# A hybrid decoder block on one core: where the first mean, the gate weights and the y combinations stand, and how the last block is closed

## Chip, core and metric

One core of one Trainium2 chip. The metric is device time in microseconds (us) of one execution; a run gives one time, and the median of the runs is used. A profiled execution gives times for every instruction of the five engines (PE: TensorE matrix unit, DVE: VectorE, ACT: ScalarE, POOL: GpSimd, SP: SyncE, which here issues nearly all DMAs).

## The reference

One layer of a decoder, sequence 2048, width 1024, float32. Cut to what matters:

```python
h = rms_norm(x, norm1_g)                       # mean of squares over the 1024 channels
z = h @ w_in                                   # 1024 -> 28 blocks of 128 channels
lru_x, lru_gate, sc_b, sc_c, sc_x = split(z)   # 8, 8, 4, 4, 4 blocks
lru_x = causal_dwconv(lru_x, 4 taps) + bias
r, i = sigmoid(lru_x @ wa + ba), sigmoid(lru_x @ wx + bx)     # 64x64 heads
log_a = -8 * r * softplus(-lam)
y_lru = scan(h = a*h + sqrt(1-a*a)*i*lru_x) * gelu(lru_gate)
y_sc  = sc_b * causal_dwconv(sc_c * sc_x, 3 taps)
x = x + concat(y_lru, y_sc) @ w_out            # 12 blocks -> 8
u = causal_dwconv(rms_norm(x, norm2_g) @ w_up, 3 taps)        # 8 -> 48 blocks
x = x + (gelu(gate) * up) @ w_down             # 24 blocks -> 8
out = rms_norm(x, final_g)
```

## The kernel before

Channels lie on the 128 partitions, positions along the free axis. The sequence is worked in two halves of 1024 positions, each half in two blocks of 512. Every product is exact to float32 by splitting both factors into a high and a low part (names `wh`/`wl` for weights, `xh`/`xl`, `fh`/`fl`, `rh`/`rl` for the other factor; ACT makes the high part at L195, DVE the low part at L196), and three matmuls take the place of one. A product of the first stage has 8 steps of 6 matmuls.

The stages follow one another on PE: products with `w_in` (`in_phase`, matmuls L234), products with `w_out` in `sweeps` (L700, tiles `ox`/`oy`), both for half 0, then both for half 1; then for each half the products with `w_up` (L581) and those with `w_down` (`sweeps` again, tiles `dx`/`dy`).

`in_phase` runs through 12 units: `L` units (a gated recurrence, two products and two small gate products `zr`, `zi`) and `S` units (short convolution, three products). In half 0 the first two products, `zin_0` and `zin_8`, go along as pieces of x arrive; then come product `zin_1`, the mean of squares of x (`inv_rms`, matmuls L265 with a matrix of ones into two PSUM banks `ms_a`, then ACT L269 and DVE L270 to L272), and `zin_9`. The result of `inv_rms`, the tile `ss_a`, scales every product when it is taken out of PSUM (`evac`, L371). The recurrence needs the constants `c8` and `nc8`, which `decay_rates` works out in some 28 operations on 128x8 numbers, with one function of ACT (`dt`).

The gate weights of a recurrence (256 columns) are loaded into the raw tile (`wr`, two buffers) of one `w_in` chunk, after that chunk, and split by `gate_weights` into a tile `gw`.

`sweeps` is one level of Strassen with seven block products: per sweep `ni/2` steps (3 for `w_out`, 6 for `w_down`), each with 24 matmuls. A step loads a weight piece and a piece of the other factor into one raw tile (L711, L712), splits both into four of the ten pages of a pool, and multiplies. The sums of blocks of y or of the FFN's inner activation that Strassen needs are made once by `combine` for each pair of units and stored to DRAM (`B11`, `B21`, `B22` are blocks, `T1` to `T4` sums; `y_d`, `f_d`). Residual tiles (`xr`, `x2r`, keys 11, 12, 21, 22) are fetched at places given by the table `at`; after a sweep DVE adds its PSUM tiles to them (L735), as `TAKEN` lists. The out-product also takes along work for the next part: in half 0 `x_prep` for the next half's x (`x_1`, `xh_1`), in half 1 `h_prep`, which prepares the FFN's input (`ha`, `hb`, `hc`, `hq`, and their parts `hhB`, `hlB`, `hhT`, `hlT`, `ht`).

At the end `finish_block` scales the last four pairs of tiles (L879) by the last mean and stores them. The last square of that mean, of the tile `x2r` with m = 3, is split and fed to two matmuls of its own.

What sets the order: PE, SP and POOL issue in the program's order. On ACT and DVE a scheduler chooses by readiness and priority (`HP` 120 before `HW` 90 before `HE` 30), and the chosen order is then fixed: each engine works in order, so an instruction that waits holds up those behind it. Buffers come from pools: 28 pages `act`, 7 pages `tmp`, 10 pages for parts, 2 raw tiles, two pairs of larger tiles, 8 PSUM banks; a new tile waits for the last reader of the page that it gets. Stores are put off by `defer(n, ...)`: `tick()`, called once for each weight load, counts down and issues what is due, on SP.

## Time and profile before

| what | us |
|---|---|
| three runs | 2307.86, 2305.12, 2307.29 |
| median | 2307.29 |
| profiled execution, whole | 2304.75 |
| its span, first to last instruction | 2302.9 |
| `w_in` products, half 0 / half 1 on PE | 7.45 to 345.2 / 461.7 to 789.9 |
| `w_out` sweeps, half 0 / half 1 | 345.2 to 461.7 / 789.9 to 910.7 |
| `w_up` and `w_down`, half 0 | 910.7 to 1368, to 1597 |
| `w_up` and `w_down`, half 1 | to 2054.5, to 2287 |

The span is what the trace covers; 1.85 us of the whole time lie around it. A line of the profile's groups reads: line of the kernel, engine, operation, output tile <- input tiles, shape, how often, time, and in brackets the idle time before it with what ended it. The chain of waits is followed back from the last instruction to what released each step.

### The profile page before, as it was taken

How to read it: one execution, taken by the hardware profiler on the slowest of the kernel's cores; microseconds unless marked ns; L12 is line 12 of the kernel's file. 1: busy time of each engine (PE TensorE's matmuls, PEld its weight loads, DVE VectorE, ACT ScalarE, POOL GpSimd, SP SyncE). 2: the span in 40 equal slices, each digit the busy share in tenths (PEclk: the TensorE clock that was granted, in tenths of full speed). 3: DMA queues.
4: the chain of work that ended last, by engine and by line, in shares of the span. 5: the costliest groups of instructions: out<-in, count | busy, mean ns of one | idle time of the engine just before them, and what ended most of it. 6: DMA issues, size and time to landing. Idle time of an engine off the chain costs nothing.

```text
span 2302.9 us, 26017 instructions
## 1 busy us (share of the span) xinstructions
PE 2272.7 (99%) x9984; PEld 1875.2 (81%) x9984; DVE 1723.8 (75%) x1910; ACT 1136.0 (49%) x1242; POOL 141.4 (6%) x232
## 2 busy tenths in 40 slices
...
GB/s 182 106 141 162 80 183 243 271 177 147 195 156 143 235 246 248 102 92 114 92 114 92 114 155 289 204 242 216 87 92 115 92 119 88 122 169 324 256 186 181
DMA packets 145597, 378.28 MB, mean 164 GB/s; under 512 B 13824, under 2 KB 17024, under 8 KB 144896
## 3 DMA queue, kind: packets, MB, share of 16 engines
...
q8 instruction: 78, 1.28, 0.2%
...
## 4 chain that ended last, share of the span: by engine, by line
PE 94%; DVE 3%; DMA 1%; ACT 1%; issue 1%; SPq 0%; DVEq 0%; ACTq 0%
PE zin_b L234 25%; PE zx L581 23%; PE zc L581 11%; PE dx L700 11%; PE dy L700 8%; PE za L581 6%; PE ox L700 5%; PE oy L700 3%; PE zr_b L234 1%; PE zi_b L234 1%; DMA x<-in_xT 1%; DMA wr_d<-sd_d_S 0%; DVE x2r L879 0%; DVE cv L294 0%; DVE fl_o L196 0%
## 5 line engine op out<-in xcount | busy, mean ns | idle before, releaser
L234 PE MATMUL zin_b<-xh,wh_in 128*128 128x512 f32 x896 | 277.2, 390 | 4.8 <-DVE ss_a L270 2.6
L234 PE MATMUL zin_b<-xl,wh_in 128*128 128x512 f32 x896 | 277.0, 390 | 0.1
L234 PE MATMUL zin_b<-xh,wl_in 128*128 128x512 f32 x896 | 276.3, 390 | 0.0
L234 PEld LDWEIGHTS zin_b<-xh,wh_in 128*128 128x128 f32 x896 | 168.5, 188 | 40.9 <-DVE ss_a L270 3.5
L234 PEld LDWEIGHTS zin_b<-xl,wh_in 128*128 128x128 f32 x896 | 168.5, 188 | 36.4 <-DVE xl L402 1.7
L234 PEld LDWEIGHTS zin_b<-xh,wl_in 128*128 128x128 f32 x896 | 168.5, 188 | 35.0
L196 DVE TENSOR_TENSOR fl_d<-wr_d,fh_d 128x1024 fp32r<-128x1024 f32 x84 | 102.8, 1223 | 104.5 <-ACT fh_d L195 102.2
L195 ACT ACTIVATE fh_d<-wr_d 128x1024 fp32r<-128x1024 f32 x84 | 89.1, 1061 | 176.7 <-PE dy L700 79.7
L196 DVE TENSOR_TENSOR wla_up<-wr_up,wha_up 128x1024 fp32r<-128x1024 f32 x48 | 58.8, 1226 | 139.0 <-ACT wha_up L195 139.0
L700 PE MATMUL dx<-fl_d,wh_d 128*128 128x512 f32 x384 | 149.5, 389 | 0.8 <-DVE fl_d L196 0.8
L700 PE MATMUL dx<-fh_d,wl_d 128*128 128x512 f32 x384 | 149.4, 389 | 0.0
L700 PE MATMUL dx<-fh_d,wh_d 128*128 128x512 f32 x384 | 149.4, 389 | 0.0
L557 DVE TENSOR_TENSOR wr_up<-wr_up 128x512 f32<-128x512 f32 x192 | 130.0, 686 | 14.7 <-DMA wr_up<-in_w_up 13.5
L195 ACT ACTIVATE wh_in<-wr_in 128x1024 fp32r<-128x1024 f32 (+1 forms) x62 | 60.2, 973 | 159.1 <-DMA wr_in<-in_w_in 154.4
L196 DVE TENSOR_TENSOR wl_in<-wr_in,wh_in 128x1024 fp32r<-128x1024 f32 (+1 forms) x62 | 69.1, 1118 | 80.4 <-ACT wh_in L195 80.4
L581 PE MATMUL zc<-hhB,whd_up 128*128 128x512 f32 x384 | 126.0, 389 | 0.0
L294 DVE SCALAR_TENSOR_TENSOR cu<-un,prm,cu 128x1024 f32<-128x1024 f32 x96 | 122.7, 1278 | 4.3 <-ACT cu L290 4.3
L196 DVE TENSOR_TENSOR wl_d<-wr_d,wh_d 128x1024 fp32r<-128x1024 f32 x84 | 102.5, 1220 | 28.0 <-ACT wh_d L195 25.6
L294 DVE SCALAR_TENSOR_TENSOR cg<-ug,prm,cg 128x1024 f32<-128x1024 f32 x96 | 122.8, 1279 | 0.4
L581 PE MATMUL zx<-ht,whc_up 128*128 128x512 f32 x384 | 118.2, 389 | 0.0
L592 ACT ACTIVATE ug<-zx 128x512 f32<-128x512 f32 x96 | 57.5, 599 | 122.8 <-PE zx L581 122.6
L195 ACT ACTIVATE wh_d<-wr_d 128x1024 fp32r<-128x1024 f32 x84 | 88.4, 1053 | 59.8 <-DMA wr_d<-sd_d_S 32.0
...
## 6 DMA issues: line engine op xcount, KB each, us to landing
wr_up<-in_w_up SPq DMA_DIRECT2D x96, 512.0 KB, 4.9
wr_in<-in_w_in SPq DMA_DIRECT2D x54, 512.0 KB, 4.1
wr_d<-sd_d_S SPq DMA_DIRECT2D x48, 512.0 KB, 3.7
wr_d<-f_d_T SPq DMA_DIRECT2D x48, 512.0 KB, 4.9
f_d_B<-cu SPq DMA_DIRECT2D x72, 256.0 KB, 2.4
wr_d<-in_w_down SPq DMA_DIRECT2D x36, 512.0 KB, 3.6
wr_d<-f_d_B SPq DMA_DIRECT2D x36, 512.0 KB, 4.6
wr_o<-so_d_S SPq DMA_DIRECT2D x24, 512.0 KB, 4.5
```

The source lines that it names most:

```text
L195: nc.scalar.activation(r32(hi), src, AF.Copy)
L196: nc.vector.tensor_tensor(r32(lo), src, hi, ALU.subtract)
L234: nc.tensor.matmul(ps[t], r32(a), r32(b[:, blk(t)]), start=(first and i == 0), stop=(last and i == 2))
L294: nc.vector.scalar_tensor_tensor(dst, src[:, k : k + T], col(o_w + k), dst, ALU.mult, ALU.add)
L557: nc.vector.tensor_tensor(raw[:, o, :], raw[:, a, :], raw[:, b, :], ALU.add)
L581: nc.tensor.matmul(ps, r32(p[:, s]), r32(self.hs[k][x][o]), start=f and i == 0, stop=l and i == 2, skip_group_check=True,)
L592: nc.scalar.activation(dst, self.x, AF.Copy)
L700: nc.tensor.matmul(ps[m], r32(p), r32(x[:, k, :]), start=first and i == 0 and n == 0, stop=(last or not on_x) and i == ni - 1 and n == 2, ...
```

## The change

It has five parts.

1. In half 0 the mean is taken inside the product `zin_1`, after two of its eight steps (`product` gets a callback `mid`). The POOL copy that marks the mean's readiness writes into a column of `dz`, the first tile of `decay_rates`, and no longer into the matrix `ones`; so `decay_rates` comes after the mean.
2. The gate weights of unit c are loaded with chunk c, not with chunk 8 + c, and split at once, before the product, into a `tmp` page and no longer an `act` page. The block sums of weights that POOL adds by DMA (`sum_step`) begin one product earlier.
3. `combine` is cut in two: `combine_even` subtracts and puts `B11` and `T1` in line for storing with the even unit of a pair, `combine_odd` does the rest with the odd unit. In `in_phase` the last odd unit's stores wait 7 ticks, where they waited 5. The FFN holds the even unit's `cg` for the sum and needs no tile `tt`.
4. In `sweeps` the residual tiles 22 are fetched where those of 12 were, and those of 12 where 22 were.
5. At the end of the last sweep the additions for m = 3 get twice the priority; `finish_block` stores each 512 positions of a channel block by itself (8 stores of 256 KB each time, where it made 4 of 512 KB); and the last square is multiplied as it is, in float32, with `ones`, without a split.

```diff
-    def decay_rates():
-        z = cp.tile([P, NLRU], F32, name="dz")
+    def decay_rates(z):
...
-    def product(ps, wts, acts):
+    def product(ps, wts, acts, mid=None):
         n = len(acts)
         for k in range(n):
+            if mid is not None and k == 2:
+                mid()
             product_step(ps, wcol(wts, k), acts[k], k == 0, k == n - 1)
...
-                nc.tensor.matmul(p, ones_r, r32(x[:, blk(b)]), start=i == 0, stop=i == len(terms) - 1)
+                w, v = (ones_r, r32(x[:, blk(b)])) if i < 2 else (ones, x[:, blk(b)])
+                nc.tensor.matmul(p, w, v, start=i == 0, stop=i == len(terms) - 1)
...
-        raw = gate_raw[c]
-        gw = flat(act(f"gw{half}_{c}"))
+        gw = flat(tmp(f"gw{half}_{c}"))
...
-        product(ps, load_weights(w_in[o], f"in{half}_{o}", o - NLRU if NLRU <= o < 2 * NLRU else None), acts)
+        c = o if o < NLRU else None
+        wts = load_weights(w_in[o], f"in{half}_{o}", c)
+        if c is not None:
+            gate_w[c] = gate_weights(c, half)
+        product(ps, wts, acts, mid)
...
-    gw = gate_weights(0, half)
-    ps_2 = in_product(1, half, acts) if half == 0 else None
-    rs = inv_rms(acc, f"a{half}", parts)
-    nc.gpsimd.tensor_copy(ones[:, 0:1], rs[:, 0:1])
-    ready.append(True)
+    def mean():
+        rss.append(inv_rms(acc, f"a{half}", parts))
+        nc.gpsimd.tensor_copy(mark, rss[0][:, 0:1])
+        ready.append(True)
+    if half == 0:
+        gate_w[0] = gate_weights(0, half)
+        ps_2 = in_product(1, half, acts, mean)
...
+        last = n >= NOUT - 2
         if n % 2 == 0:
-            put(y_d[half], 5 if n < NOUT - 2 else 4, n // 2, "B11", y[:, blk(0)])
-            even = y
+            even, yc = y, flat(tmp(f"yc{half}_{n}"))
+            combine_even(y_d[half], 4 if last else 5, n // 2, even, yc)
         else:
-            combine(y_d[half], 5, n // 2, even, y, c, d)
+            combine_odd(y_d[half], 7 if last else 5, n // 2, even, y, yc, flat(tmp(f"yd{half}_{n}")))
...
+    def combine_even(dst, when, i, a, c):
+        put(dst, when, i, "B11", a[:, t0])
+        nc.vector.tensor_tensor(c[:, t0], a[:, t0], a[:, t1], ALU.subtract)
+        put(dst, when, i, "T1", c[:, t0])
...
-    ("12", ((1, 0), (1, 0))), ("22", ((1, 1), (1, 2)))
+    ("22", ((1, 0), (1, 0))), ("12", ((1, 1), (1, 2)))
...
-                    with tc.high_priority(offset=HP if last else HE):
+                    with tc.high_priority(offset=HE if not last else 2 * HP if m == 3 else HP):
...
-                    scaled(r[:, m, :], 4 * mh + 2 * p + m, rs)
-                c = 4 * mh + 2 * p
-                o = T + t * NB
-                defer(4, yT[c : c + 2, :, o : o + NB].rearrange("m p c -> p m c"), r)
+                    c = 4 * mh + 2 * p + m
+                    scaled(r[:, m, :], c, rs)
+                    defer(4, yT[c, :, T + t * NB : T + (t + 1) * NB], r[:, m, :])
...
-                terms.extend(mean_split(sq, "l2"))
+                terms.append(sq)
```

How the instructions stand, at three places. First, ACT in the first stage of half 0, around the mean of x (`wh_in_9` is the high part of chunk 9's weights, `cv_0` and `xch_0` belong to the convolution of the first recurrence); before:

```order
L195 ACTIVATE wh_in_9_606<-wr_in_9_605 128x1024
L195 ACTIVATE wh_in_20_715<-wr_in_20_714 128x1024
L269 ACT_TABLE_LOAD
L269 ACTIVATE ry_a_545<-ms_a_0_539,eps 128x512
L269 ACTIVATE ry_a_545<-ms_a_512_540,eps 128x512
L195 ACTIVATE wh_in_24_818<-wr_in_24_817 128x1024
L292 ACTIVATE cv_0_558<-xl_0_553,prm 128x1024
L195 ACTIVATE wh_in_16_882<-wr_in_16_881 128x1024
L195 ACTIVATE xch_0_563<-cv_0_558 128x1024
L195 ACTIVATE wh_in_2_948<-wr_in_2_947 128x1024
```

and now:

```order
L196 ACTIVATE gw_1_493<-wr_in_1_486 128x256
L274 ACT_TABLE_LOAD
L274 ACTIVATE ry_a_514<-ms_a_0_508,eps 128x512
L274 ACTIVATE ry_a_514<-ms_a_512_509,eps 128x512
L196 ACTIVATE wh_in_9_611<-wr_in_9_610 128x1024
L196 ACTIVATE wh_in_20_721<-wr_in_20_720 128x1024
L196 ACTIVATE wh_in_24_820<-wr_in_24_819 128x1024
L297 ACTIVATE cv_0_564<-xl_0_559,prm 128x1024
L159 ACT_TABLE_LOAD
L159 ACTIVATE dt<-dz 128x8
L196 ACTIVATE wh_in_16_884<-wr_in_16_883 128x1024
L196 ACTIVATE wh_in_2_950<-wr_in_2_949 128x1024
```

`gw_1`'s split, which stood far behind these rows, and the mean's `ry_a` now stand ahead of `wh_in_9`; the load of a function table and `dt` of `decay_rates` come in behind `cv_0`, and `wh_in_2` now stands ahead of `xch_0`, which is the next row.

Second, the queue SP in half 0's out-product, around the end of the first sweep (`wr_o_1_1` is the raw tile of sweep 1, step 1; `yc_11`, `sv_3`, `yd_11` hold the last pair of y); before:

```order
L711 DMA wr_o_1_1_2755<-so_d_S_1_212 128x1024
L712 DMA wr_o_1_1_2755<-y_d_T_1_95 128x1024
L192 DMA y_d_T_2_96<-yc_11_2579 128x512
L192 DMA y_d_T_2_99<-yc_11_2579 128x512
L192 DMA y_d_B_2_90<-sv_3_2574 128x512
L192 DMA y_d_T_2_102<-yd_11_2580 128x512
L192 DMA y_d_B_2_93<-sv_3_2574 128x512
L192 DMA y_d_T_2_105<-yd_11_2580 128x512
L509 DMA xr_22_0_2772<-in_xT 128x2x512
L400 DMA x_1_2798<-in_xT 128x1024
L711 DMA wr_o_1_2_2807<-so_d_S_2_213 128x1024
L712 DMA wr_o_1_2_2807<-y_d_T_2_96 128x1024
```

and now:

```order
L527 DMA xr_22_0_2728<-in_xT 128x2x512
L527 DMA xr_22_1_2730<-in_xT 128x2x512
L730 DMA wr_o_1_1_2756<-so_d_S_1_213 128x1024
L731 DMA wr_o_1_1_2756<-y_d_T_1_96 128x1024
L527 DMA xr_12_0_2767<-in_xT 128x2x512
L408 DMA x_1_2793<-in_xT 128x1024
L730 DMA wr_o_1_2_2802<-so_d_S_2_214 128x1024
L731 DMA wr_o_1_2_2802<-y_d_T_2_97 128x1024
L527 DMA xr_12_1_2813<-in_xT 128x2x512
L730 DMA wr_o_2_0_2847<-so_d_S_0_215 128x1024
L731 DMA wr_o_2_0_2847<-y_d_T_0_98 128x1024
L193 DMA y_d_T_2_100<-yc_10_2445 128x512
```

`x_1` and the loads of step 2 (`wr_o_1_2`) and of `wr_o_2_0` moved ahead of five stores of the last pair; the sixth (`T1`) has gone out earlier. DVE at the end of that sweep before (additions L735 of its PSUM tiles `oy`):

```order
L196 TENSOR_TENSOR fl_o_2_0_2860<-wr_o_2_0_2852,fh_o_2_0_2859 128x1024
L735 TENSOR_TENSOR xr_12_0_2727<-xr_12_0_2727,oy_1_0_2712 128x512
L735 TENSOR_TENSOR xr_22_0_2772<-xr_22_0_2772,oy_1_0_2712 128x512
L735 TENSOR_TENSOR xr_12_0_2727<-xr_12_0_2727,oy_1_1_2713 128x512
L735 TENSOR_TENSOR xr_12_1_2729<-xr_12_1_2729,oy_1_2_2714 128x512
L196 TENSOR_TENSOR wl_o_2_1_2900<-wr_o_2_1_2896,wh_o_2_1_2899 128x1024
L196 TENSOR_TENSOR fl_o_2_1_2904<-wr_o_2_1_2896,fh_o_2_1_2903 128x1024
L735 TENSOR_TENSOR xr_22_0_2772<-xr_22_0_2772,oy_1_1_2713 128x512
```

and now (L754):

```order
L197 TENSOR_TENSOR fl_o_2_0_2860<-wr_o_2_0_2847,fh_o_2_0_2859 128x1024
L754 TENSOR_TENSOR xr_12_0_2767<-xr_12_0_2767,oy_1_0_2713 128x512
L754 TENSOR_TENSOR xr_12_0_2767<-xr_12_0_2767,oy_1_1_2714 128x512
L754 TENSOR_TENSOR xr_22_0_2728<-xr_22_0_2728,oy_1_0_2713 128x512
L754 TENSOR_TENSOR xr_22_0_2728<-xr_22_0_2728,oy_1_1_2714 128x512
L754 TENSOR_TENSOR xr_12_1_2813<-xr_12_1_2813,oy_1_2_2715 128x512
L754 TENSOR_TENSOR xr_12_1_2813<-xr_12_1_2813,oy_1_3_2716 128x512
L754 TENSOR_TENSOR xr_22_1_2730<-xr_22_1_2730,oy_1_2_2715 128x512
L754 TENSOR_TENSOR xr_22_1_2730<-xr_22_1_2730,oy_1_3_2716 128x512
L410 SCALAR_TENSOR_TENSOR xl_2_2889<-x_2_2887,prm,xh_2_2888 128x1024
L197 TENSOR_TENSOR wl_o_2_1_2900<-wr_o_2_1_2896,wh_o_2_1_2899 128x1024
L197 TENSOR_TENSOR fl_o_2_1_2904<-wr_o_2_1_2896,fh_o_2_1_2903 128x1024
```

All eight additions and `xl_2` now stand ahead of `wl_o_2_1`, where four additions did.

Third, ACT in half 1's out-product, around sweep 1, step 2; before:

```order
L195 ACTIVATE fh_o_1_1_5940<-wr_o_1_1_5927 128x1024
L195 ACTIVATE hhB_1_5912<-ha_1_5900 128x1024
L195 ACTIVATE hhB_1_5916<-hb_1_5901 128x1024
L195 ACTIVATE hhT_1_5920<-hc_1_5906 128x1024
L195 ACTIVATE ht_1_5924<-hq_1_5907 128x512
L195 ACTIVATE wh_o_1_2_5973<-wr_o_1_2_5970 128x1024
L195 ACTIVATE fh_o_1_2_5977<-wr_o_1_2_5970 128x1024
```

and now:

```order
L196 ACTIVATE fh_o_1_1_5935<-wr_o_1_1_5928 128x1024
L196 ACTIVATE hhB_1_5913<-ha_1_5901 128x1024
L196 ACTIVATE wh_o_1_2_5968<-wr_o_1_2_5965 128x1024
L196 ACTIVATE hhB_1_5917<-hb_1_5902 128x1024
L196 ACTIVATE fh_o_1_2_5972<-wr_o_1_2_5965 128x1024
L196 ACTIVATE hhT_1_5921<-hc_1_5907 128x1024
L196 ACTIVATE wh_o_2_0_6018<-wr_o_2_0_6010 128x1024
```

The four parts of `h_prep`'s tiles stood together ahead of step 2's splits; now one stands ahead of `wh_o_1_2` and one between it and `fh_o_1_2`.

More of the change, by code (lines that the diff above doesn't have):

```diff
@@ L99, in block_kernel @@
     xl_halo = cp.tile([P, NLRU, 3], F32, name="xl_halo")
+    dz = cp.tile([P, NLRU], F32, name="dz")
+    mark = dz[:, 0:1]
     h_last = cp.tile([P, NLRU], F32, name="h_last")
@@ L203, in block_kernel @@
     gate_raw = {}
+    gate_w = {}
     def load_parts(src, name, parts, gate=None):
@@ L313, in gate_weights @@
     def gate_weights(c, half):
-        raw = gate_raw[c]
-        gw = flat(act(f"gw{half}_{c}"))
+        gw = flat(tmp(f"gw{half}_{c}"))
         hi, lo = gw[:, 0 : 2 * P], gw[:, 2 * P : 4 * P]
         with tc.high_priority(offset=HW):
-            split(hi, lo, raw)
+            split(hi, lo, gate_raw[c])
         return hi, lo
@@ L414, in in_phase @@
             acts = []
-            loads = [load_parts(w_in[o], f"in{half}_{o}", KC // 2, g) for o, g in ((0, None), (NLRU, 0))]
+            loads = [load_parts(w_in[o], f"in{half}_{o}", KC // 2, g) for o, g in ((0, 0), (NLRU, None))]
             wts = [None, None]
@@ L431, in in_phase @@
         parts = mean_split(acc, f"a{half}")
-        gw = gate_weights(0, half)
-        ps_2 = in_product(1, half, acts) if half == 0 else None
-        rs = inv_rms(acc, f"a{half}", parts)
-        nc.gpsimd.tensor_copy(ones[:, 0:1], rs[:, 0:1])
-        ready.append(True)
+        rss = []
+        def mean():
[5 more added lines that the diff above has]
+            ps_2 = in_product(1, half, acts, mean)
+        else:
+            ps_2 = None
+            mean()
+        rs = rss[0]
         xc, cv = lru_conv(0, half, pss[0], rs)
         if half == 0:
-            decay_rates()
+            decay_rates(dz)
         cur = (xc, cv, lru_gate(0, half, pss[1], rs))
@@ L450, in in_phase @@
                 ps_g = in_product(NLRU + nxt[1], half, acts) if n == 0 else None
-                if n > 0:
-                    gw = gate_weights(c, half)
-                gates = lru_gates(c, half, xc, gw)
+                gates = lru_gates(c, half, xc, gate_w[c])
                 if nxt[0] == "L":
```

20 lines of the change are left out of this document (9 added, 11 removed).

## The prediction

> **What bounds the kernel now.** I read the page's head and its chain first.
>
> ```profile
> span 2302.9 us, 26017 instructions
> PE 2272.7 (99%) x9984; PEld 1875.2 (81%) x9984; DVE 1723.8 (75%) x1910; ACT 1136.0 (49%) x1242; POOL 141.4 (6%) x232
> PE 94%; DVE 3%; DMA 1%; ACT 1%; issue 1%; SPq 0%; DVEq 0%; ACTq 0%
> ```
>
> PE is the bound in every stage. One row of the chain in order of time gives its pace, and one of the view of waits (total, number, longest) what mostly stops it.
>
> ```profile
> 78.81 54.40 PE zin_b L234 x240
> ```
>
> ```profile
> PE oy L700 <- DVE fl_o L196: 3.9, 3, 1.6
> ```
>
> At full pace 240 matmuls take 54.40 us, 0.2267 us each. The change takes one matmul of some 9,770 away, so only the places where PE waits can give anything. Below, a loss at a place is the distance between the starts of two matmuls less 0.2267 us, read from PE's timeline, with the slower matmul or two behind it. All such losses add up to some 24 us; work elsewhere that becomes cheaper is worth nothing.
>
> **First stage of half 0** (parts 1 and 2).
>
> ```profile
> 10.05 1.15 ACT L401 ACTIVATE xh<-x,prm 128x1024 fp32r<-128x1024 f32 x1 [0.48 <-DMA x<-in_xT]
> 11.39 0.18 DVE dt L174
> 11.75 1.29 DVE xl L402
> 13.08 30.33 PE zin_b L234 x130
> 43.41 0.69 PE ms_a L265 x3
> 44.19 1.28 ACT L269 ACT_TABLE_LOAD   x1 [4.81 <-PE ms_a L265]
> 46.20 1.30 DVE ss_a L270 x2
> 46.95 1.09 PE L234 MATMUL zin_b<-xh,wh_in 128*128 128x512 f32 x2 [2.64 <-DVE ss_a L270]
> 59.82 0.73 PE L234 MATMUL zr_b<-xch,gw 128*128 128x512 f32 x2 [1.34 <-ACT xch L195]
> 61.08 0.74 PE L234 MATMUL zr_b<-xcl,gw 128*128 128x512 f32 x2 [0.53 <-DVE xcl L196]
> 68.19 1.23 DVE L196 TENSOR_TENSOR xcl<-cv,xch 128x1024 fp32r<-128x1024 f32 x1 [1.13 <-ACT xch L195]
> 75.34 0.40 ACT L195 ACTIVATE gw<-wr_in 128x256 fp32r<-128x256 f32 x1
> 75.79 0.73 PE L234 MATMUL zr_b<-xch,gw 128*128 128x512 f32 x2 [1.23 <-ACT gw L195]
> ```
>
> - Start: `decay_rates` holds DVE in small operations of 0.18 us; without them `xl` of the second x piece starts at 11.2, when `xh` is done, and not at 11.75. PE hangs on it at 13.08: −0.6.
> - `zin_9` waits for a PSUM bank that the mean has to free: 3.3 lost at 46.95 (2.80, and 0.5 in the slow matmuls after it). Now the mean's matmuls come 36 matmuls, 8.2 us, earlier, and PE has 8.2 us of `zin_1` to do while ACT and DVE work on them. That chain took 3.3 us, from 44.1 to the end of `ss_a` L270 at 47.5. The wait goes: −3.3.
> - `zr_0` lost 2.4 in two waits for the parts of the convolution (`xch`, `xcl`). From the mean's matmuls (44.2) to `xcl_0` (61.0) the chain takes 16.9. With the mean ending at 35.7 (`zin_1` starts at 43.41 − 10.88 − 0.6 = 31.9, then two steps of 1.36 and 4 matmuls, and 0.2 to the end) it would be done at 52.6. But the 28 operations of `decay_rates`, one more table load of ACT (1.28) and one weight split now stand in it. All of DVE's added work would be 28 × 0.18 = 5.0; part of it fills pauses in which DVE waits for ACT. I take 2.7, `xcl_0` at 55.3. PE wants it at 43.41 − 0.6 + 0.9 + 10.88 + 0.45 = 55.0: 0.4 to 0.5 stay, −1.9. With nothing in the way it is −2.4, with all of it 0.
> - `zr_1` lost 1.5 (1.40 and 0.11), waiting for `gw_1`, whose split ACT reached at 75.34. It is now split before the mean. What is late next is `xcl_1`, at 69.4 before and by the same 5.7 earlier now, 63.7, plus some decay work, against PE's 54.6 + 0.5 + 2.72 + 10.88 = 68.7. It is in time: −1.5.
>
> Sum: **−7.2** (7.3, rounded toward the work added on DVE), between −4.2 (the first rival) and −8.0. Behind 78.81 PE keeps its pace through the rest of both first stages, so the earlier `gw` splits (0.40 each on ACT, their number unchanged) and the earlier `T1` gain nothing there. They cost nothing as long as the weights stay several products ahead and the seven `tmp` pages come free in time.
>
> **Out-product, half 0** (part 3).
>
> ```profile
> 361.11 7.55 DMA x<-in_xT
> 372.73 0.50 PE L700 MATMUL oy<-fh_o,wh_o 128*128 128x512 f32 x1 [0.17 <-ACT fh_o L195]
> 374.62 0.51 PE L700 MATMUL oy<-fl_o,wh_o 128*128 128x512 f32 x1 [1.38 <-DVE fl_o L196]
> 378.12 2.48 DVE L735 TENSOR_TENSOR xr<-xr,oy 128x512 f32<-128x512 f32 x4 [0.55 <-PE oy L700]
> 380.52 1.22 DVE L196 TENSOR_TENSOR wl_o<-wr_o,wh_o 128x1024 fp32r<-128x1024 f32 x1
> ```
>
> Step 2 of sweep 1 loses 0.33 + 1.66 + 0.12 = 2.1: its split stands on ACT behind `xh_1`, whose load was issued behind six stores. Five of these now stand behind the loads of this step and the next, so `x_1` is issued and lands earlier by the time of five issues: −2.1. Behind it a new wait arises. After the sweep DVE took four additions (2.48) ahead of `wl_o_2_1`; now eight (4.95) and `xl_2` (1.2). Started 1.9 us before the sweep's end, where they started here too, then 1.14 and 1.22 for the two splits, `fl_o_2_1` is ready at −1.9 + 4.95 + 1.2 + 1.14 + 1.22 = 6.6 after the end; PE needs it at 5.44 + 0.23 = 5.7. That costs 1.0 (0 if DVE gets a microsecond earlier to its additions, 2.1 if as much is lost here as at the place before). Net **−1.0**, between −2.1 and 0.
>
> **Out-product, half 1** (parts 3 and 4).
>
> ```profile
> 812.82 0.50 PE L700 MATMUL oy<-fl_o,wh_o 128*128 128x512 f32 x1 [0.90 <-DVE fl_o L196]
> 818.83 0.50 PE L700 MATMUL oy<-fh_o,wh_o 128*128 128x512 f32 x1 [0.50 <-ACT fh_o L195]
> 820.92 0.80 PE L700 MATMUL oy<-fl_o,wh_o 128*128 128x512 f32 x1 [1.59 <-DVE fl_o L196]
> 815.00:820.00 5.00, 3.83 (x16) 2.62 (x14) 5.00 (x6) 5.00 (x7) 0.00 (x0) 1.00 0.47 181
> 820.00:825.00 5.00, 4.08 (x12) 3.25 (x13) 3.14 (x3) 1.47 (x2) 0.00 (x0) 0.66 0.63 221
> ```
>
> ```profile
> L195 ACT ACTIVATE fh_d<-wr_d 128x1024 fp32r<-128x1024 f32 x84 | 89.1, 1061 | 176.7 <-PE dy L700 79.7
> ```
>
> (The windows' columns: PE, PEld, DVE, ACT, POOL busy, granted clock, DMA share, GB/s.) The wait at 812.82 stays: DVE's order ahead of it is the same. The second place loses 0.66 + 1.87 in waits, and the matmuls behind them run slowly, 0.37 + 6 × 0.2 more, together 3.9 to 4.1, of which I count 3.9. ACT and DVE were both full from 815 to 820 with the four parts of `h_prep`'s tiles ahead of step 2's splits. Now two stand ahead on ACT, one before each split. Counting the new order's rows from the same start, ACT's at the 1.06 of the last row and DVE's at 1.22, `fl_o_1_2` comes at 819.1 instead of 820.9; PE needs it at 818.2: 0.8 stay, with no slow clock behind so short a wait as the 0.90 at 812.82, which ran at 1.00 after. **−3.1**, between 0 and −3.9.
>
> [...]
>
> **Down, half 1** (part 3).
>
> ```profile
> 2060.00:2065.00 5.00, 5.00 (x23) 4.13 (x22) 4.96 (x5) 2.96 (x3) 0.00 (x0) 1.00 0.22 46
> 2075.00:2085.00 10.00, 10.00 (x46) 8.29 (x45) 4.00 (x4) 3.19 (x3) 0.00 (x0) 1.00 1.04 399
> 2105.41 0.50 PE L700 MATMUL dy<-fl_d,wh_d 128*128 128x512 f32 x1 [0.76 <-DVE fl_d L196]
> ```
>
> One step loses 1.5 (0.38 + 1.03 + 0.11), because its load lands late in a stretch in which the DMA runs full. `T1` of the last pair, 256 KB, moves from that burst to the even unit, into 2060 to 2065, where the share is 0.22. At 399 GB/s it is 0.26 MB / 0.399 = 0.65 us less ahead of the load: **−0.6**, between 0 and −1.5.
>
> **End** (part 5).
>
> ```profile
> 2287.95 0.64 ACT sq_last L913
> ...
> 2290.02 0.51 PE ms_l L265
> 2293.45 5.39 DVE L879 SCALAR_TENSOR_TENSOR x2r<-x2r,prm,ss_l 128x512 f32<-128x512 f32 x8
> 2294.89 4.35 SPq L192 DMA_DIRECT2D out_yT<-x2r  x4
> out_yT<-x2r SPq DMA_DIRECT2D x4, 512.0 KB, 2.9
> f_d_B<-cu SPq DMA_DIRECT2D x72, 256.0 KB, 2.4
> 1.00 4.54 PE L746 MATMUL warm<-ones 128*128 128x128 f32 x22 [1.00 <-POOL eps L96]
> ```
>
> From the square's end (2288.59) to the last mean's matmul (2290.53) lie 1.94. In its place stands one float32 matmul. The only such row is the last, at the start of the kernel: 11 of a quarter of the columns (two records each) in 4.54 us, 0.41 each, so 4 × 0.41 + 0.28 = 1.9 at that pace. At the pace of this kernel's matmuls, four times 0.2267 and the 0.28 that the row of 0.51 has over it, it is 1.2; I take that, since PE worked until 2286.5: −0.7, between 0 and −1.0. The doubled priority changes no order on DVE and gives nothing. The stores: the first now waits for one scaled tile of 0.67, not two, and eight issues at 4.35 / 8 or so, if an issue took half as long for half the bytes, keep up with DVE's 5.39 us: −0.7, between 0 and −0.8. **−1.4** together.
>
> **Sum:** −7.2 − 1.0 − 3.1 − 0.6 − 1.4 = −13.3. The profiled execution took 2304.75 (its span 2302.9 and 1.85 around it), which gives 2291.45. It lies 2.5 below the median of the runs, 2307.29; against that the sum gives **2294.0**.
>
> **Rivals.**
> - The first stage gives part of it back: the decay operations all lie in the way of `xcl_0`, so `zr_0` gains nothing (−5.4), and `zin_20` waits for one weight split of 1.2 behind them. Then −4.2 in place of −7.2: 2297.0. For it: from 46.2 to 61.0 DVE or what waits on it is already last in the chain. Against it: DVE has pauses there, and only `zr_0` is near its limit.
> - The sweeps give nothing: the stall moves from sweep 1 to sweep 2, and `h_prep` still has to be done on the same engines in the same stretch. Then −13.3 + 4.1 = −9.2, 2298.1. For it: DVE full from 815 to 820. Against it: ACT's order puts step 2's splits earlier.
> - Slower: `gw` in a `tmp` page. ACT works in order, and if the page's last reader is a store (of `yc` or `yd`) not landed yet, the split stops ACT, and with it the weights. It decides if the page comes free later than the weights' lead, over one product of 10.88. Eight units at a store's 2.4 us (the row of `f_d_B<-cu`) are +19; with −13.3 the time is about 2313. Against it: those stores stand on SP before the loads of the chunk concerned.
> - Stores one by one: if each of the last stores had its whole time to landing for itself, eight at 2.4 would take 19.2 against 11.6 for four at 2.9, 7.6 more: 2301.6. Against it: four of 2.9 were issued within 4.35 us, and the end lay 8 us behind the first issue, so they overlapped. [...]
> - No effect: the waits are merely taken over by the next operand everywhere. The doubled priority is of that kind. Within 4.6 us of no change.
>
> **Chances.** Forecast 0.54 (2290 to 2297.5); first stage 0.2; sweeps 0.12; stores 0.02; nothing 0.08; slower 0.04. All better ends together are −17.3, 2290.0, and the three runs of before lie 2.7 apart, some 1.4 to a side: 2288.5 is the range's lower end. The first two rivals together give −6.2, 2301: its upper end. Within it lie the forecast and these two, 0.86 in all. A measurement of this kernel can tell about 0.2%, 4.6 us, from no change: faster than 2302.7 has 0.88, within 0.08, slower 0.04.
>
> **What would show it.** In the changed profile: no wait of `zin_b` for `ss_a` near 44 and none of `zr_b` for `gw`; the second gate products near 68.5; a short wait of `oy` near 385 in half 0; one wait under 1 us near the second step in half 1; `ms_l` as one longer record and the last stores starting one tile after scaling begins. A wait of ACT for a DMA ahead of a `gw` split, or losses within the first stages after 70 us, would prove the sum wrong.

## The result, and the profile after

| | before | changed |
|---|---|---|
| median of six runs, us | 2307.43 | 2293.58 |
| lowest to highest | 2302.71 to 2309.76 | 2291.88 to 2296.08 |
| ratio, 95% interval | | 0.9944 (0.9932 to 0.9957) |
| profiled execution, us | 2304.75 | 2291.88 |
| its span, us | 2302.9 | 2290.1 |

The changed kernel is faster by 13.85 us, 0.6%. The profiled executions differ by 12.87, their spans by 12.8. The page's head, its chain (shares by engine) and, behind the marks, two rows of the view of waits (total, number, longest) of the changed kernel read:

```profile
span 2290.1 us, 26044 instructions
PE 2268.6 (99%) x9984; PEld 1873.6 (82%) x9984; DVE 1722.5 (75%) x1909; ACT 1137.2 (50%) x1242; POOL 153.4 (7%) x232
PE 88%; DVE 3%; DMA 1%; ACT 1%; issue 1%; POOL 0%; DVEq 0%; SPq 0%; ACTq 0%; POOLq 0%
...
PE oy L719 <- DVE fl_o L197: 1.5, 2, 0.9
...
PE zr_b L236 <- ACT xch L196: 1.0, 1, 1.0
```

PE is still the bound, and its busy time fell by only 4.1 us (some of the slow matmuls are gone); the rest of the 12.8 was waiting. The wait of `oy` for `fl_o` went from 3.9 us in three places to 1.5 in two. A wait of `zr_b` for `xch` is left, but not the one that the prediction spoke of, as its place in the timeline shows. Where the time went is read from the starts of the same work on PE in the two timelines:

| work on PE | before | changed | earlier by | step |
|---|---|---|---|---|
| first product after `zr_1`, `zi_1` | 78.64 | 71.27 | 7.4 | |
| first product after `zr_4`, `zi_4` | 217.36 | 212.07 | 5.3 | −2.1 |
| half 0, out-product | 345.20 | 339.91 | 5.3 | 0 |
| half 0, its sweep 4 | 412.60 | 406.30 | 6.3 | +1.0 |
| half 1, out-product | 789.78 | 783.50 | 6.3 | 0 |
| half 0, up | 910.57 | 899.92 | 10.7 | +4.4 |
| half 1, down | 2054.81 | 2044.23 | 10.6 | 0 |
| end of the last mean | 2290.51 | 2278.19 | 12.3 | +1.7 |
| end of the span | 2302.94 | 2290.11 | 12.8 | +0.5 |

PE's timeline of the changed kernel at the places of the steps (start, duration, instruction, and in brackets the idle time before it and what ended it):

```profile
34.95 0.61 PE L270 MATMUL ms_a<-rh_a,ones_r 128*128 128x512 f32 x2
54.90 0.62 PE L236 MATMUL zr_b<-xch,gw 128*128 128x512 f32 x2
55.36 0.63 PE L236 MATMUL zr_b<-xcl,gw 128*128 128x512 f32 x2
...
208.41 0.73 PE L236 MATMUL zr_b<-xch,gw 128*128 128x512 f32 x2 [0.98 <-ACT xch L196]
209.67 0.73 PE L236 MATMUL zr_b<-xcl,gw 128*128 128x512 f32 x2 [0.53 <-DVE xcl L197]
...
379.19 0.50 PE L719 MATMUL ox<-fl_o,wh_o 128*128 128x512 f32 x1 [0.81 <-DVE fl_o L197]
...
812.91 0.50 PE L719 MATMUL oy<-fl_o,wh_o 128*128 128x512 f32 x1 [0.62 <-DVE fl_o L197]
...
2093.74 0.50 PE L719 MATMUL dy<-fl_d,wh_d 128*128 128x512 f32 x1 [0.17 <-DVE fl_d L197]
```

The mean's matmuls at 34.95 and both products of `zr_0` start without waiting: the three early stalls are gone. At 208.41 and 209.67 stands a **new stall**, before `zr_4`; with the slower matmul behind each it loses 1.14 + 0.11 + 0.70 + 0.11 = 2.1 us. Before, PE did not wait there. The other rows are the waits that the prediction left standing: 0.97 + 0.11 lost at 379.19, 0.78 + 0.11 at 812.91, 0.33 + 0.11 at 2093.74.

DVE ahead of the wait at 379.19:

```profile
370.71 4.95 DVE L754 TENSOR_TENSOR xr<-xr,oy 128x512 f32<-128x512 f32 x8 [1.31 <-PE oy L719]
375.58 1.28 DVE L410 SCALAR_TENSOR_TENSOR xl<-x,prm,xh 128x1024 fp32r<-128x1024 f32 x1
376.78 1.22 DVE L197 TENSOR_TENSOR wl_o<-wr_o,wh_o 128x1024 fp32r<-128x1024 f32 x1
377.92 1.22 DVE L197 TENSOR_TENSOR fl_o<-wr_o,fh_o 128x1024 fp32r<-128x1024 f32 x1
```

Eight additions, `xl`, then the two splits: `fl_o` ends at 379.14 and PE starts at 379.19. These are the four operations, in that order, from which the prediction worked out its 1.0.

Half 1's out-product, the two windows that hold the work of 815 to 825 in the kernel before, which now comes 6.3 us earlier (PE, PEld, DVE, ACT, POOL busy; granted clock; DMA share; GB/s), and two rows of ACT at their start:

```profile
808.70:813.70 5.00, 4.38 (x19) 3.30 (x18) 5.00 (x5) 4.75 (x6) 0.00 (x0) 1.00 0.88 318
813.70:818.70 5.00, 5.00 (x23) 4.11 (x22) 5.00 (x8) 1.06 (x2) 0.00 (x0) 1.00 0.97 329
```

```profile
807.13 1.06 ACT L196 ACTIVATE hhB<-ha 128x1024 fp32r<-128x1024 f32 x1 [6.27 <-DVE ha L548]
808.10 1.04 ACT L196 ACTIVATE wh_o<-wr_o 128x1024 fp32r<-128x1024 f32 x1
```

DVE and ACT are about as full as before in the first window (5.00 and 4.75 of 5; both were 5.00), so there is about as much work in the stretch. What is new is the order: the split `wh_o` of step 2 follows the first of `h_prep`'s four parts and not the last. The clock stays at 1.00.

The end, rows of the chain in order of time, and behind the marks the rows of DVE and SP for the scaling and the stores:

```profile
2276.38 0.64 ACT sq_last L931
2277.07 1.14 PE ms_l L270 x2
...
2281.13 5.39 DVE L898 SCALAR_TENSOR_TENSOR x2r<-x2r,prm,ss_l 128x512 f32<-128x512 f32 x8
2281.91 4.97 SPq L193 DMA_DIRECT2D out_yT<-x2r  x8
```

The float32 matmul takes 1.14 us, and the first store is issued 0.78 after scaling begins, where it was 1.44.

How the new stall comes about is read backwards on three engines. ACT in order, before `zr_4`:

```profile
201.05 1.06 ACT L196 ACTIVATE wh_in<-wr_in 128x1024 fp32r<-128x1024 f32 x1 [5.53 <-DMA wr_in<-in_w_in]
202.01 1.23 ACT L297 ACTIVATE cv<-xl,prm 128x1024 f32<-128x1024 f32 x1
...
207.30 1.06 ACT L196 ACTIVATE xch<-cv 128x1024 fp32r<-128x1024 f32 x1 [4.06 <-DVE cv L299]
```

`xch_4` ends just before PE takes it. Ahead of it ACT stood idle for 5.53 us at `wh_in_14`, waiting for a load, with the convolution `cv_4` queued behind. SP (weight loads L215, stores L193):

```profile
158.68 0.33 SPq L193 DMA_DIRECT2D y_d_T<-yc  x1
...
162.08 9.96 SPq L215 DMA_DIRECT2D wr_in<-in_w_in  x2
...
182.10 9.22 SPq L215 DMA_DIRECT2D wr_in<-in_w_in  x2
...
194.51 0.33 SPq L215 DMA_DIRECT2D wr_in<-in_w_in  x1
```

and DVE's gate splits:

```profile
181.57 0.42 DVE L197 TENSOR_TENSOR gw<-wr_in,gw 128x256 fp32r<-128x256 f32 x1
194.07 0.42 DVE L197 TENSOR_TENSOR gw<-wr_in,gw 128x256 fp32r<-128x256 f32 x1
```

There are two raw tiles. The load for `wh_in_14` is issued at 194.51, two hundredths after the split of `gw_5` ended (194.07 + 0.42): the tile that it goes to held the gate weights of unit 5 until then. The load of chunk 13 at 182.10 follows in the same way on `gw_4`, in the other tile (181.57 + 0.42); as that tile was held so long, the two loads ahead, of chunks 12 and 5, both went through the tile that unit 5's weights then held, 162.08 and 171.71. And the load of chunk 12 stood on SP behind the stores that begin at 158.68, which wait for the third recurrence. So a chain of recurrences, stores, loads and gate splits, each waiting for the one before, now ends last at `zr_4`.

### The profile page after: what moved, and what is told of

Its sections match the earlier page's. It is cut to its first block, busy times and chain, and to the rows that moved or that the text cites. A ratio compares the mean times of both kernels' runs of the same rounds, so it can differ in the third digit from the quotient of the medians.

```text
span 2290.1 us, 26044 instructions
## 1 busy us (share of the span) xinstructions
PE 2268.6 (99%) x9984; PEld 1873.6 (82%) x9984; DVE 1722.5 (75%) x1909; ACT 1137.2 (50%) x1242; POOL 153.4 (7%) x232
## 4 chain that ended last, share of the span: by engine, by line
PE 88%; DVE 3%; DMA 1%; ACT 1%; issue 1%; POOL 0%; DVEq 0%; SPq 0%; ACTq 0%; POOLq 0%
PE zx L599 23%; PE zin_b L236 19%; PE zc L599 11%; PE dx L719 11%; PE dy L719 8%; PE za L599 6%; PE ox L719 5%; PE oy L719 4%; DMA wr_in<-in_w_in 1%; PE zi_b L236 1%; PE zr_b L236 1%; DMA wr_d<-f_d_T 1%; DVE x2r L898 0%; DVE r L350 0%; DVE xr L754 0%
```

## The experiments

Each experiment starts from the changed kernel unless it says otherwise. Two questions lead. Why does PE stall at `zr_4`: because a raw tile is held by a late gate split (R), or because the chain starts late, for instance behind the decay operations (D), which now stand at the head of the first recurrence? And which edits are the named gains owed to? The letters S, V, O and F in the expectations stand for rivals: S of R, V of D, O and F of one another. Kernels e8 and e9 were run five times each, the others once; of those the places on PE say more than the total, as the six runs of the changed kernel lie 4.2 us apart and those of the kernel before 7.1.

**e1: gate weights loaded into a page of their own.** The raw tile has no second reader.

```diff
-            if gate is not None and i == 0:
-                gate_raw[gate] = tile_[:, 4, : 2 * P]
-                nc.sync.dma_start(gate_raw[gate], w_gate[gate])
...
+        raw = flat(tmp(f"gr{half}_{c}"))[:, : 2 * P]
+        nc.sync.dma_start(raw, w_gate[c])
```

> The changed kernel with one edit: the gate weights are loaded into a tmp page of their own, not into the raw tile of chunk c. Theory R (raw tile): the changed kernel's one new stall, zr_4 waiting 1.14 + 0.70 us near 208 us for xch_4 and xcl_4, comes from the late split of gw_4 and gw_5, which holds the raw tile, so that chunks 13 and 14 load late and wh_in_14 stands waiting ahead of cv_4 on ACT. Then no wait over 0.3 us at zr_4, and PE's losses up to 340 us fall by about 2. Rival S (stores): the chunks load late because SP waits at the stores of the y pairs that stand ahead of them; then zr_4 still loses 1.5 to 2.1.

It took 2306.22 us, beside 2309.50 for the kernel before. PE's timeline:

```profile
207.38 0.62 PE L233 MATMUL zr_b<-xch,gw 128*128 128x512 f32 x2
...
237.84 1.22 PE L233 MATMUL zin_b<-xh,wh_in 128*128 128x512 f32 x2 [3.10 <-ACT wh_in L196]
```

and ACT's:

```profile
235.30 1.24 ACT L294 ACTIVATE cv<-xl,prm 128x1024 f32<-128x1024 f32 x1 [7.12 <-DVE xl L378]
```

The stall at `zr_4` is gone, as R has it, but the run doesn't isolate R: its schedule came out otherwise. The first scan starts at 79.46 (85.33 in the changed kernel), and ACT has `cv_4` ahead of `wh_in_14`. And the kernel loses more elsewhere. Each recurrence now takes a second `tmp` page for its gate weights, and ACT has `cv_6`, which waits 7.12 for its input, ahead of `wh_in_14`: PE loses 3.26 in one wait for these weights, and the kernel some 12 us against the changed one. e11, below, does the same for one unit alone.

**e2: part 2 undone** (gate weights with chunk 8 + c, split late, in an `act` page).

```diff
-        gw = flat(tmp(f"gw{half}_{c}"))
+        gw = flat(act(f"gw{half}_{c}"))
...
+                if n > 0:
+                    gate_w[c] = gate_weights(c, half)
```

> The changed kernel with part 2 undone: gate weights come with chunk 8 + c, are split in the unit that uses them, into an act page. By the prediction's term the wait of zr_1 for gw_1 comes back: 1.0 to 1.6 us near 69 us. Theory R: the stall at zr_4 near 208 goes (under 0.3), so PE's losses up to 340 us are about the changed kernel's or 0.5 less. Rival S: zr_4 still loses about 2, and the losses are 1.5 more. A rival to the prediction's term: with the mean earlier ACT reaches gw_1 in time anyway, and zr_1 does not wait.

It took 2296.34. On PE:

```profile
69.40 0.73 PE L236 MATMUL zr_b<-xch,gw 128*128 128x512 f32 x2 [0.57 <-ACT gw L196]
259.54 0.73 PE L236 MATMUL zr_b<-xch,gw 128*128 128x512 f32 x2 [2.16 <-ACT gw L196]
```

The wait of `zr_1` for `gw_1` comes back, smaller than before and than expected (0.84 lost, where it was 1.5). The stall at `zr_4` goes, although the load of chunk 14 is issued only at 213.45: here ACT's order has `cv_4` and `xch_4` right behind `wh_in_13`, so that `zr_4` hangs on no later load. But `zr_6` and `zr_7` now wait for their gate weights (the row at 259.54 is `zr_6`), and behind `zr_6`'s 2.16 eight matmuls are slow, 1.6 together. At the end of the first stage the kernel stands 3.9 us behind the changed one (343.82 against 339.91). Part 2 is worth 3.9 net of the stall at `zr_4` in this one run, not the 1.5 of `zr_1`.

**e3: the mean behind `zin_1` again**, all else as changed.

```diff
-            ps_2 = in_product(1, half, acts, mean)
+            ps_2 = in_product(1, half, acts)
+            mean()
```

> The changed kernel with the mean taken behind the whole of zin_1, as before; decay_rates and the gate weights stay as changed. By the prediction's terms zin_9 waits for ss_a again, 3.2 to 3.4 us near 47, and zr_0 for xch_0 and xcl_0 2.4 or, with decay_rates in that chain, up to 4; zr_1 does not wait for gw_1. PE stands 5.5 to 7.5 later than in the changed kernel at the end of zr_1. Rival: the mean's place is worth only the 3.3 of zin_9, since zr_0 has its own chain; then 3.3 later.

It took 2299.20. PE's timeline:

```profile
46.70 1.39 PE L236 MATMUL zin_b<-xh,wh_in 128*128 128x512 f32 x2 [2.64 <-DVE ss_a L275]
...
61.11 0.73 PE L236 MATMUL zr_b<-xch,gw 128*128 128x512 f32 x2 [1.69 <-ACT xch L196]
```

`zin_9` waits for the mean as before, with slow matmuls behind, and `zr_0` for the convolution. `zr_1` starts at 77.45, 8.9 later than in the changed kernel: 4.5 at `zin_9` with the slow matmuls, 3.0 at `zr_0`, 1.6 in slow matmuls behind it (less 0.1 elsewhere). `zr_4` loses only 0.5 here, and at the end of the first stage 7.4 are left. At `zr_1` that is more than expected.

**e4: part 4 undone** (residual tiles 12 fetched first again).

```diff
-... ("22", ((1, 0), (1, 0))), ("12", ((1, 1), (1, 2))) ...
+... ("12", ((1, 0), (1, 0))), ("22", ((1, 1), (1, 2))) ...
```

> The changed kernel with part 4 undone (tiles 12 fetched first, 22 after them). Theory O (order of stores): the second stall of half 1's out-product fell from 3.9 to 0.9 because the stores of the last pair stand behind the loads of step 2; then it stays at 0.9 here, and the 0.6 + 0.5 near 893 of the kernel before stay away. Rival F (fetch order): the residual tiles that SP waited for, 8.3 us at 785.7 in the kernel before, delayed h_prep; then the stall is 2.5 to 4 again and the losses of 0.5 at the start of sweep 6 come back.

It took 2300.18. ACT in half 1's out-product, and the window behind the place of the second stall:

```profile
812.14 1.06 ACT L196 ACTIVATE hhB<-ha 128x1024 fp32r<-128x1024 f32 x1 [6.27 <-DVE ha L548]
...
815.00 0.61 ACT L196 ACTIVATE ht<-hq 128x512 fp32r<-128x512 f32 x1
815.52 1.05 ACT L196 ACTIVATE wh_o<-wr_o 128x1024 fp32r<-128x1024 f32 x1
```

```profile
820.00:825.00 5.00, 5.00 (x23) 4.13 (x22) 3.71 (x6) 0.99 (x1) 0.00 (x0) 1.00 0.92 334
```

The second stall of half 1 is back (0.66 lost at 817.57, 1.86 at 819.66), but no slow clock follows. ACT's order is the old one again: all four parts of `h_prep`'s tiles stand ahead of step 2's `wh_o`. The loads of step 2 had landed by 807.9, so the split waits for its turn on ACT and not for the DMA. At the down-product 0.93 + 1.03 + 0.11 are lost. Of the 8.3 us by which this profile is longer than the changed kernel's, 4.8 lie at `zr_4`, which this edit doesn't touch (see e8).

**e5: the store order of part 3 and the float32 square undone** (the last odd unit's stores at 5 ticks; the last square split).

```diff
-                combine_odd(y_d[half], 7 if last else 5, n // 2, even, y, yc, ...)
+                combine_odd(y_d[half], 5, n // 2, even, y, yc, ...)
...
-                terms.append(sq)
+                terms.extend(mean_split(sq, "l2"))
```

> The changed kernel with two edits undone that lie far apart in time: the last odd unit's stores of y wait 5 ticks again, not 7, and the last square is split into two parts with a matmul each. First: in half 0's out-product x_1 is loaded behind the stores, so step 2 of sweep 1 loses about 2 us near 367, and the 1.0 at 379 goes or stays; in half 1 the second stall is 2 to 4 again if the place of the stores decides it, 0.9 if the fetch order does. Second: from the end of sq_last to the last ry_l 1.9 to 2.0 us instead of 1.2.

It took 2301.37, beside 2306.42 for the kernel before. At `zr_4` 6.1 are lost (see e8). In half 0 the old stall is back, 0.33 at 371.47 and 1.66 at 373.35, and the wait at 379 is gone. From the last square's end to the first operation that reads the mean pass 1.98, where the changed kernel has 1.22. Half 1's window behind the second stall:

```profile
820.00:825.00 5.00, 5.00 (x16) 3.95 (x15) 0.98 (x2) 1.06 (x1) 0.00 (x0) 0.66 0.57 211
```

Here too the second stall is back (0.66 and 1.86), though the fetch order is the new one, and this time with a granted clock of 0.66 behind it. ACT's order is that of e4, and step 2's loads had landed by 812.2, over 3 us ahead of its first split at 815.55. With e4 this says: **the gain in half 1 needs both edits**, the order of the fetches and that of the stores, because only with both does the scheduler put `wh_o` behind the first part. Why it does so no run shows. Neither of the two theories, that one of the edits alone gives the gain, holds.

**e6: the down-product's part of 3 and the eight stores undone** (the last pairs' `T1` of the FFN stored with the odd unit; four stores of 512 KB at the end).

```diff
-            combine_even(f_d[half], when, j // 2, cu, cg)
+            put(f_d[half], when, j // 2, "B11", cu[:, blk(0)])
+            nc.vector.tensor_tensor(cg[:, blk(0)], cu[:, blk(0)], cu[:, blk(1)], ALU.subtract)
...
+            put(f_d[half], when, j // 2, "T1", c[:, blk(0)])
...
-                    defer(4, yT[c, :, T + t * NB : T + (t + 1) * NB], r[:, m, :])
+                defer(4, yT[c : c + 2, :, o : o + NB].rearrange("m p c -> p m c"), r)
```

> The changed kernel with two edits undone: T1 of the FFN is stored with the odd unit (subtracted with the even one), and finish_block makes 4 stores of 512 KB each time. First: the wait at sweep 1, step 3 of the last down phase is 1.5 us again, not 0.4. Rival: the 0.4 comes from elsewhere (the rest of the program earlier), then it stays. Second: from the first scaled tile to the end of the span 9.4 to 9.7 us as before, instead of 9.0; if the stores overlap fully with their landing, the same 9.0.

It took 2292.76. Its chain at the end:

```profile
2281.52 5.39 DVE L900 SCALAR_TENSOR_TENSOR x2r<-x2r,prm,ss_l 128x512 f32<-128x512 f32 x8
2282.96 4.35 SPq L193 DMA_DIRECT2D out_yT<-x2r  x4
```

From the first scaled tile to the end of the span it takes 9.47, the changed kernel 8.98: the eight stores are worth 0.5, in one run. The step of the down-product loses 0.94, neither the 1.5 nor the 0.4 of the expectation. That is within what kernels with the early `T1` and the new fetch order lose there (0.3 to 1.3 in ten profiles: 0.3 in e1, 0.4 in the changed kernel, 1.3 in e7 and e8), so the earlier `T1` is not shown to be what helped. The two kernels with the old fetch order, before and e4, lost 1.5 and 2.1. That may point to part 4; no run shows why.

**e7 and e8: the decay operations ahead of the mean.** They stand after the x pieces and before the mean's chain. The kernel was run once (e7) and then five times (e8), with the changed kernel (**e9**) beside it.

```diff
         if half == 0:
+            decay_rates(dz)
             gate_w[0] = gate_weights(0, half)
...
-        if half == 0:
-            decay_rates(dz)
```

> The changed kernel with decay_rates before the mean, so that its 28 small operations run at the start, as in the kernel before. By the prediction's term PE reaches zin_1 0.6 later than in the changed kernel; by the changed profile, where the start gained only 0.1, 0.1 later. zr_0 and zr_1 do not wait in either case. If the time at zr_1 is the same within 0.1, moving decay_rates was worth nothing.

> The kernel of run e7 again (the changed kernel with decay_rates before the mean), timed. In e7 the stall at zr_4 was absent and the end of the first stage 1.7 us earlier than in the changed kernel. Theory D (decay): decay_rates inside the first unit's chain makes the whole serial chain of scans, stores and weight loads up to zr_4 some 2 us later, and without it zr_4 does not wait; then the stall is under 0.5 again, and the median lies 1.5 to 5 us below the changed kernel's on the same chip. Rival V (variation): e7 was a lucky execution, since kernels with the same order in the first stage lost between 1.9 and 4.8 there; then zr_4 loses 1 to 5 and the medians agree within 1 us.

> The changed kernel itself, timed on the same chip beside run e8. Both theories: 2292 to 2296 us. Theory D: a loss of 1.5 to 5 us at zr_4 as in four profiles so far; theory V: anything from 0 to 5.

| on one chip | median, us | lowest to highest | ratio to before (95%) |
|---|---|---|---|
| before, nine runs | 2305.29 | 2301.82 to 2311.61 | |
| e9, the changed kernel, five runs | 2294.39 | 2293.34 to 2295.89 | 0.9952 (0.9937 to 0.9968) |
| e8, decay first, five runs | 2290.86 | 2290.18 to 2292.37 | 0.9936 (0.9922 to 0.9950) |

e7 took 2291.18. The two sets of five don't overlap, and e8 is 3.5 us below e9. e8's timeline of SP, where the changed kernel's was shown above:

```profile
156.67 0.33 SPq L193 DMA_DIRECT2D y_d_T<-yc  x1
...
160.09 9.49 SPq L215 DMA_DIRECT2D wr_in<-in_w_in  x2
...
179.65 9.37 SPq L215 DMA_DIRECT2D wr_in<-in_w_in  x2
...
192.21 0.33 SPq L215 DMA_DIRECT2D wr_in<-in_w_in  x1
```

Each link is there, at the same distances (from chunk 12 to chunk 14 32.1, against 32.4), but the whole chain stands 2.0 to 2.5 us earlier. Its head is on ACT; e8 and the changed kernel:

```profile
65.60 1.28 ACT L342 ACT_TABLE_LOAD   x1
```

```profile
67.13 1.28 ACT L342 ACT_TABLE_LOAD   x1 [0.87 <-DVE nc L177]
```

In the changed kernel the first recurrence's ACT function waits 0.87 for `nc8`, the last result of `decay_rates`; in e8 `nc8` is long there. The schedule behind it also comes out a little otherwise, and the first scan on DVE, in e8 and in the changed kernel, starts 2.65 apart:

```profile
82.68 2.28 DVE L350 TENSOR_TENSOR_SCAN r<-a,i 128x1024 f32<-128x1024 f32 x1
```

```profile
85.33 2.28 DVE L350 TENSOR_TENSOR_SCAN r<-a,i 128x1024 f32<-128x1024 f32 x1
```

Seven profiles have the mean inside `zin_1` and the same order of these instructions on ACT. By the loss at `zr_4`, with the slow matmuls behind it, they fall into two groups:

| run | first scan | load of chunk 14 | split `wh_in_14` | lost at `zr_4` |
|---|---|---|---|---|
| e7 | 83.07 | 192.63 | 199.2 | 0 |
| e8 | 82.68 | 192.21 | 199.7 | 0.7 |
| changed | 85.33 | 194.51 | 201.0 | 2.1 |
| e9 | 84.78 | 193.86 | 201.1 | 4.3 |
| e6 | 85.73 | 194.54 | 201.2 | 1.9 |
| e5 | 85.25 | 195.70 | 202.8 | 6.1 |
| e4 | 85.54 | 195.87 | 203.7 | 6.9 |

Decay first, the chain starts some 2 us earlier and 0 to 0.7 is lost (the expectation said under 0.5); decay last, 1.9 to 6.9, though the first stage of these five is the same code. Inside the second group the start of the scan doesn't order the loss; the split of `wh_in_14` very nearly does, and 1.6 to 2.1 of the loss in e9, e5 and e4 lie in slow matmuls behind the waits. The load of chunk 14 takes 6.5 to 7.8 us to land in these seven; what makes it vary no run shows. D holds: the rival V had the medians within 1 us. In the profiles of e9 and e8 the first stage's end lies 3.0 us apart (341.56 and 338.52) and the whole span only 1.8, since e8 loses some 0.5 and 0.9 more at two later places. `zr_1` pays nothing that can be told for the operations at the new place: it starts at 68.89 in e7 and 68.50 in e8, against 68.55, 67.96 and 68.89 in the changed kernel, e9 and e6, which have them last.

**e10: e8's kernel with the mean behind `zin_1`.** Does D explain why e3 cost more than expected?

```diff
+            decay_rates(dz)
             gate_w[0] = gate_weights(0, half)
-            ps_2 = in_product(1, half, acts, mean)
+            ps_2 = in_product(1, half, acts)
+            mean()
```

> The kernel of e8 with the mean behind zin_1 again: the price of the mean's place alone, without decay_rates in its chain. By the prediction's terms zin_9 waits 3.3 and zr_0 some 2.4 (two waits, for xch_0 and xcl_0), zr_1 not: PE 5.5 to 6 later at the end of zr_1 than in e8. In e3, with decay_rates in the chain, it was 8.9. Rival: 8 or more here too, so that the mean's place and not decay_rates makes the larger part.

It took 2298.38, 7.5 above e8's median.

`zr_0` waits the same 1.69 us for `xch_0` as in e3 (at 61.73), and `zin_9` the same 2.64 for `ss_a`. So the decay operations cost nothing at `zr_0`. `zr_1` starts 7.95 later than in e8: 4.7 at `zin_9` with the slow matmuls behind it, 3.0 at `zr_0`, the rest before the mean. That is nearly the 8 of the rival: D doesn't explain why e3 cost more than expected, the mean's place does. The mean's place alone is worth 7.7 here, and up to 9.0 where more slow matmuls follow (e3).

**e11: the gate weights of unit 5 in half 0 alone loaded into a page of their own.** The chain starts as in the changed kernel, and one raw tile has its late reader no more.

```diff
-            if gate is not None and i == 0:
+            if gate is not None and i == 0 and name.startswith("in0_") and gate in (5,):
+                gate_raw[gate] = flat(tmp(f"gr_{name}"))[:, : 2 * P]
+                nc.sync.dma_start(gate_raw[gate], w_gate[gate])
+            elif gate is not None and i == 0:
```

> The changed kernel, but the gate weights of unit 5 in half 0 alone are loaded into a page of their own, so that the raw tile of chunk 5 comes free with the split of its weights (wl_in_5, which ended at 179.6 in the changed kernel) and not with gw_5 (194.49). The decay operations stay where the change put them, so the chain starts as late as in the changed kernel (first scan between 84.8 and 85.8, chunk 12's load between 160.9 and 162.9). Theory R (the late reader of the raw tile delays the loads): chunk 14's load is issued when wl_in_13 is done, 28.5 to 30 us after chunk 12's and not 32.4, and zr_4 loses less than 0.7. Rival S (the late start of the chain sets it, and the held tile adds nothing): chunk 14's load still follows 32 us behind chunk 12's, and zr_4 loses 1.9 or more. ACT's order puts wh_in_14 behind cv_4 here, so the issue times decide and not the wait alone. In all 2290 to 2293 by R, 2293 to 2296 by S.

It took 2290.51, beside 2303.00 for the kernel before. SP, and then PE:

```profile
163.93 9.49 SPq L215 DMA_DIRECT2D wr_in<-in_w_in  x2
...
183.49 1.27 SPq L215 DMA_DIRECT2D wr_in<-in_w_in  x2
...
193.08 0.33 SPq L215 DMA_DIRECT2D wr_in<-in_w_in  x1
```

```profile
207.86 0.62 PE L239 MATMUL zr_b<-xch,gw 128*128 128x512 f32 x2
```

The chain starts even later than in the changed kernel (first scan at 85.89, chunk 12 at 163.93, not 162.08), and yet chunk 14 goes out 1.4 earlier: 29.2 behind chunk 12, where it was 32.4 (32.1 to 33.4 in the seven profiles above). Chunk 6 now goes out right behind chunk 13, as `gw_5` no longer holds the tile of chunk 5. `zr_4` loses nothing. **R holds** for the 3.2 us between the loads. That the stall goes altogether is owed in part to two other things: the load of chunk 14 lands 4.4 us after its issue, where it took 6.5, and ACT takes `wh_in_14` behind `cv_4`. So the stall had two causes of about the same size, the start of the chain (D, some 2 us) and the held tile (R, 3.2); without the first most or all of it goes, and without the second it went in the one run that there is.

## Why the prediction was right

It came out right: 2294.0 forecast, 2293.58 measured, and faster. But the first stage gave 1.9 less than forecast and half 1's two products together 1.8 more, so the sum is better than its parts by luck. Term by term, in the profiled executions:

| term | forecast | measured |
|---|---|---|
| first stage of half 0 | −7.2 | −5.3 |
| out-product, half 0 | −1.0 | −1.0 |
| out-product, half 1 | −3.1 | −4.4 |
| down-product, half 1 | −0.6 | −1.1 |
| end | −1.4 | −1.3 |
| sum | −13.3 | −12.8 (with 0.3 of scatter and rounding between) |

- **First stage.** To the end of `zi_1` the forecast held, −7.4 for −7.2. Inside it the start gave 0.1, not 0.6, and even that can't be told from scatter: `zr_1`, behind it, starts between 67.96 and 68.89 in the profiles with this start (changed, e9, e6). The `xl` that PE hangs on was no longer behind `dt`, but its `xh` began at 10.42, not 10.05, after a longer wait for the load (1.10 us), and PE lost 0.74 + 0.12 at 12.95. `zin_9` gave its 3.3, and `zr_1` its 1.5. `zr_0` gave all of its 2.4, where 1.9 was forecast: `xcl_0` ended at 55.15, as forecast (55.3), and only the missing half microsecond at the start put PE's need behind it. A term that was missing altogether is the stall at `zr_4`. What failed is the step "Behind 78.81 PE keeps its pace through the rest of both first stages", and the condition behind it, that the earlier splits "cost nothing as long as the weights stay several products ahead". The weights did stay ahead of PE's own products. The operand that came late was the convolution's, which stood on ACT behind a weight split whose load was late, for the two reasons that e8 and e11 show: the chain of recurrences started some 2 us later than it could have, and a raw tile had got a late reader (3.2). Undoing the first is worth 3.5 us between the medians of e9 and e8. The prediction had named losses after 70 us as a sign that its sum would be wrong, and for this stage the sign was right.
- **The mean's place** is worth 7.7 to 9.0 us up to `zr_1` (e10, e3), more than the 5.2 that the forecast gave to `zin_9` and `zr_0`. Part 2's worth in the forecast was the 1.5 of `zr_1`; e2 puts it at 3.9, since without it `zr_6` and `zr_7` come to wait for their gate weights once the mean no longer holds PE back. That is a price of the new pace, which the timeline of before couldn't show.
- **Out-product, half 0.** The mechanism and the size were right: 2.1 goes, and 1.1 comes back at an operand of sweep 2. In e5 both are as they were.
- **Out-product, half 1.** The second stall's −3.1 came out as −3.2. The additional −1.2 was not foreseen: two waits of before, at 893.77 (0.54 + 0.11) and at 899.78 (0.44 + 0.11), late in the stage, are gone. They stay nearly away in e4 (0.19) and e5 (0.27) also, so neither edit of the order brings them back alone. Their cause stays open. The prediction ascribed the stall to the place of `h_prep`'s tiles on ACT, and worked out `fl_o_1_2` at 819.1 in the old times; it came at 812.86, 6.3 earlier, as everything here. In e4 and e5 the old order and the old stall come together, which bears the mechanism out. The prediction did not say that either edit alone would leave the stall as it was.
- **Down, half 1.** The size came out larger and the reason is not borne out: e6, without the earlier `T1`, loses 0.5 more than the changed kernel, but kernels that have it lose up to 1.3 there, more than e6. Whether this term was earned or luck stays open.
- **End.** The float32 square was forecast at −0.7 and gave −0.76 (1.97 to 1.22). The factor of four in the 1.2 us behind it stands in no row of before; the changed kernel's one float32 matmul took 1.14, about 4 × 0.2267 + 0.23, which bears it out. The stores were forecast at −0.7 and gave −0.5: eight issues took 4.97, not 4.35. The doubled priority was not undone by itself; DVE's last additions and splits stand in the order of before, as forecast.
- **Rivals.** The first rival, that the decay operations lie in the way, had the right operations and the wrong place: they cost nothing that shows at `zr_0` (e10 waits there as e3 does), and some microseconds at `zr_4`, 150 us later. The slower case did not come: no `gw` split on ACT or DVE has idle time before it. The stores ran one over the other: eight issues within 4.97 us, and the end of the span 8.2 us behind the first.
